# Query, key and value order in group B, and layer 0's key/value projection slice by slice

## The chip, the cores and the metric

The kernel runs on one core of one Trainium2 chip, in one launch. The metric is the device time of a run in microseconds (us), the median of several runs. Five engines work side by side, each through its own queue in order: TensorE (PE in the profile, its weight loads PEld), VectorE (DVE), ScalarE (ACT), GpSimd (POOL) and SyncE (SP), which here only issues DMA transfers. They meet at semaphores.

## The reference

A two-layer encoder on a sequence of 512 tokens and 1024 features, all in float32. A layer is:

```
h = rmsnorm(x, g_attn)
qa, ka, va, qb, kb, vb = split(h @ w_in)          # 512, 128, 128, 512, 512, 512 columns
ya = windowed_attention(rope(norm(qa)), rope(norm(ka)), va, sink)   # 8 heads of 64, 2 kv heads
yb = differential_attention(rope(norm(qb)), rope(norm(kb)), vb)     # 4 heads, two softmaxes each
x = x + concat(ya, rmsnorm(yb)) @ w_out
h = rmsnorm(x, g_ffn)
gate, val = split(h @ w_up)                       # 2 x 2816 columns
x = x + (silu(conv3(gate)) * val) @ w_down
```

## The kernel before, in words

x lies transposed: features on the 128 partitions, in eight slices of 128 (`x_sb[k]`), tokens along the free axis. Every product is made from three float32r products: each operand is split into a high part `hi` (rounded by ScalarE) and a low part `lo` (the rest, by VectorE or GpSimd), and `mm3` (L197 to L200) adds hi·hi, hi·lo and lo·hi in PSUM. Weights come in units of at most 512 KB. `emit_unit` (L176) loads one into `wr`, rounds it into `wh` and writes the rest into `wl`; `next_unit` (L190) keeps the loads three units ahead. There are two buffers `wr` and three each of `wh` and `wl`.

The norm before a projection is not applied to x. `Norm.add` (L212) multiplies a slice by its gain and splits it into `na_h` and `na_l`; `Norm.square` (L221) sums the squares of the slices; `Norm.rms` (L233) sums them over the partitions with plain float32 matmuls (`na_ss`) and GpSimd raises the mean to the power -0.5 (`na_r`, `r_tok`). The scale of a token is multiplied in when a projection's bank is read: `scaled` (L329) for queries and keys, `v_out` (L374) for values.

The input projection of a layer runs in nine chunks of 256 columns (`CHUNKS`, L29): key/value of group A, two of A's queries, and for each half of group B value, query and key. `project` (L315) works through a chunk in two banks of two token tiles each, so 8 x 12 = 96 matmuls. After a bank of queries or keys, `qk_out` (L335) does the head norm and the rotary embedding: ScalarE scales and squares, VectorE sums, GpSimd takes the power, multiplies and adds, TensorE transposes into the one bank `tq`, and ScalarE and VectorE split the result. It works in four shared buffers `rp`. The banks in PSUM are: two `mm`, two `at`, one double bank `sc` for scores, one `acc` and one `tq`.

At the start of layer 0 (L254 to L269) the eight slices of x and the first two weight units are loaded, eight `add` are emitted and then eight `square`: four on GpSimd, four on ScalarE and VectorE. Then come the tables for the rotary embedding (`make_tabs`, on GpSimd) and `rms`, then chunk after chunk.

Attention is a track of its own. `attend` (L592) goes through group A's eight steps (two score groups each), then through eight score steps for each half of B; values follow a step or two behind, and after a half's four value products the outputs are normed (`b_norm`: `ss_yb`, `rt_yb`, both in `tq`). `weave` (L125) interleaves this track with the other one, B's projections (`proj_b`, L629) and the first output projection, by given shares of cost. A track may hand out a condition and is passed over until it holds: B's scores of a half wait for `("done", half)`, set when its projections are emitted. The order in which the instructions then stand in the engines' queues is chosen by a planner from the emission order and its own estimate of times.

The feed-forward part follows (L697 to L741).

Of the kernel before, what the change touches and what calls it, by code (L numbers as in the profile page):

```python
# [10 lines left out]
F32 = mybir.dt.float32  # L11
# [17 lines left out]
CHUNKS = ("akv", "aq0", "aq1", "bv0", "bq0", "bk0", "bv1", "bq1", "bk1")  # L29
# [7 lines left out]
FIRST_SQ = 4  # L37
# [5 lines left out]
def kernel(  # L43
# [102 lines left out]
    ones, nhalf, warm = (unit[:, i:i + 1] for i in range(3))  # L146
    nc.gpsimd.memset(ones, 1.0)
    nc.gpsimd.memset(nhalf, -0.5)

# [26 lines left out]
    def emit_unit():  # L176
# [7 lines left out]
        for o in ([slice(0, k)] if i > 1 else [slice(j, j + 1) for j in range(k)]):  # L184
            nc.scalar.copy(hi[:, o], raw[:, o])  # L185
            eng.tensor_tensor(out=lo[:, o], in0=raw[:, o], in1=hi[:, o], op=ALU.subtract)  # L186
        ready.append((hi, lo))
        state["emitted"] += 1

# [13 lines left out]
    class Norm:  # L203
        def __init__(self, l, base, name):
            self.l, self.base, self.name = l, base, name
            self.first = l == 0 and base == 0
            self.x = []
            self.hi = [None] * NK
            self.lo = [None] * NK
            self.part = [sb.tile([P, S], F32, tag="tab", bufs=3, name=f"{name}_sum")]  # L210
# [10 lines left out]
        def square(self, k):  # L221
            if self.first and k == FIRST_SQ:
                self.part.append(tmp(f"{self.name}_sum2"))
            sq = self.part[-1] if k == 0 or self.first and k == FIRST_SQ else tmp(f"{self.name}_q{k}")
            if self.first and k < FIRST_SQ:
                nc.gpsimd.tensor_tensor(out=sq, in0=self.x[k], in1=self.x[k], op=ALU.mult)
            else:
                nc.scalar.activation(sq, self.x[k], AF.Square)
            if sq is not self.part[-1]:
                eng = nc.vector if self.first and k >= FIRST_SQ else nc.gpsimd  # L230
                eng.tensor_tensor(out=self.part[-1], in0=self.part[-1], in1=sq, op=ALU.add)

        def rms(self):  # L233
            acc = accum(f"{self.name}_ss")
            for t in range(NT):
                for k, sq in enumerate(self.part):
                    nc.tensor.matmul(acc[:, t:t + 1], lhsT=sq[:, t * P:(t + 1) * P], rhs=ones,  # L237
                                     start=k == 0, stop=k == len(self.part) - 1)
# [11 lines left out]
    def split_out(hi, lo, src):  # L250
        nc.scalar.copy(hi, src)
        nc.vector.tensor_tensor(out=lo, in0=src, in1=hi, op=ALU.subtract)
# [18 lines left out]
    for l in range(depth):  # L271
# [36 lines left out]
        r_tok = norm.rms()  # L308
        if l == 0:
            make_tabs((2, 3))  # L310
# [4 lines left out]
        def project(name, done, alloc):  # L315
            w = [next_unit(), next_unit()]
            for tp in range(NT // 2):
                bank = alloc(f"pj{l}_{name}_{tp}").rearrange("p (t c) -> p t c", t=2)
                for i in range(2):
                    t = 2 * tp + i  # L320
                    for k in range(NK):
                        mm3(bank[:, i], (h_in.hi[k][:, t * P:(t + 1) * P], h_in.lo[k][:, t * P:(t + 1) * P]),
# [6 lines left out]
        def scaled(name, bank, tp):  # L329
            raw = rp(name)  # L330
            for i in range(2):
                nc.scalar.activation(raw[:, i], bank[:, i], AF.Copy, scale=r_tok[:, 2 * tp + i:2 * tp + i + 1])
# [56 lines left out]
        run(project("akv", akv_done, turn))  # L389
# [10 lines left out]
        run(proj_a(0, turn))  # L400
        run(proj_a(1, turn))
# [88 lines left out]
        def bv_done(half, bank, tp):  # L490
            v = keep(f"vb{l}_{half}_{tp}")
            vb[half, tp] = (v[:, 0], v[:, 1])
            for i in range(2):
                o = slice(i * CW, (i + 1) * CW)
                v_out(bank[:, i], v[:, 0, o], v[:, 1, o], 2 * tp + i)
# [96 lines left out]
        def attend():  # L592
# [4 lines left out]
            def values():  # L597
# [9 lines left out]
                if qb % 2:  # L607
                    yield from b_values(kind, qb // 2, j)
# [202 lines left out]
```

## Time and profile before

| | |
|---|---|
| median of 3 runs | 1282.15 us (1281.47 to 1282.38) |
| profiled execution | 1282.14 us, span 1280.4 us |
| TensorE busy | 1226.6 us, 96% of the span |
| VectorE, ScalarE, GpSimd busy | 58%, 44%, 28% |
| mean granted TensorE clock | 0.98 of full speed |
| read from memory | 99.73 MB, 80 GB/s over the span |

Busy time of TensorE counts a matmul from its start to its modelled end, and neighbours overlap; the idle time between them is what to look at. In a row of the timeline, the note in brackets is the time for which the engine stood idle before it, and what ended that.

### The profile page before, as it was taken

To read this page: it belongs to the slowest core of one execution; us is meant where nothing else is said; L and a number is where in the kernel's file an instruction comes from. 1 tells how busy PE (TensorE), PEld (TensorE's weight loads), DVE (VectorE), ACT (ScalarE), POOL (GpSimd) and SP (SyncE) were. 2 spreads that over 40 slices of the span, in tenths; PEclk is the share of its full clock that TensorE was granted. 3 is DMA by queue.
4 is the path that set the end of the run, shared out by engine and by line. 5 is a ranking of instruction groups with operands and counts; after the bars stand their busy time and mean duration, and the time that the engine had idled before them with its cause. 6 is when DMAs were issued, how large, how long until landed. Compare 5 with 4: busy or idle time off the path is not lost. (4 is left out here: it accounts for less than half of the span.)

```text
span 1280.4 us, 17034 instructions
## 1 busy us (share of the span) xinstructions
PE 1226.6 (96%) x6648; PEld 1034.8 (81%) x6648; DVE 737.5 (58%) x1181; ACT 569.6 (44%) x1007; POOL 359.2 (28%) x354
## 2 busy tenths in 40 slices
PE   6999996989999999999999999978999999999998
PEld 6988875787888888888899988757888888888887
DVE  6656786767655324554447677766765542355532
ACT  4477854435433223333345877544443332233321
POOL 5756481114211000112146465702421110011100
PEclk8999998899999999999999999979999999999999
DMA  5312120113332233332332112201133323333232
GB/s 176 100 35 66 42 78 22 32 34 100 99 99 87 87 107 99 99 99 72 93 115 67 52 49 67 64 3 37 63 108 106 98 76 99 107 99 99 80 109 91
DMA packets 32752, 102.92 MB, mean 80 GB/s; under 512 B 3872, under 2 KB 4128, under 8 KB 32672
## 3 DMA queue, kind: packets, MB, share of 16 engines
q1 hardware_dynamic: 32672, 101.84, 25.9%
q8 instruction: 52, 0.85, 0.3%
q14 instruction: 28, 0.23, 0.1%
HBM read 99.73 MB, written 2.10 MB: 80 GB/s over the span
## 5 line engine op out<-in xcount | busy, mean ns | idle before, releaser
L185 ACT CAST wh<-wr 128x1024 fp32r<-128x1024 f32 (+3 forms) x210 | 197.8, 945 | 404.0 <-PE up L199 171.0
L199 PE MATMUL up<-nf_l,wh 128*128 128x512 f32 x704 | 274.6, 390 | 0.6 <-DVE nf_l L217 0.5
L200 PE MATMUL up<-nf_h,wl 128*128 128x512 f32 x704 | 274.1, 390 | 0.4
L198 PE MATMUL up<-nf_h,wh 128*128 128x512 f32 x704 | 273.4, 390 | 0.0
L186 DVE TENSOR_TENSOR wl<-wr,wh 128x1024 fp32r<-128x1024 f32 (+3 forms) x174 | 192.2, 1108 | 107.0 <-ACT wh L185 106.7
L717 POOL TENSOR_TENSOR cv<-cv,rb 128x512 f32<-128x512 f32 x44 | 59.2, 1346 | 516.8 <-ACT cv L716 516.8
L199 PEld LDWEIGHTS up<-nf_l,wh 128*128 128x128 f32 x704 | 132.1, 188 | 30.0 <-DVE nf_l L217 2.8
L200 PEld LDWEIGHTS up<-nf_h,wl 128*128 128x128 f32 x704 | 132.2, 188 | 28.5 <-DVE wl L186 1.5
L198 PEld LDWEIGHTS up<-nf_h,wh 128*128 128x128 f32 x704 | 132.1, 188 | 27.6 <-ACT nf_h L216 0.2
L200 PE MATMUL dn<-act,wl 128*128 128x512 f32 x352 | 139.0, 396 | 0.0
L198 PE MATMUL dn<-act,wh 128*128 128x512 f32 x352 | 137.4, 391 | 0.0
L199 PE MATMUL dn<-act,wh 128*128 128x512 f32 x352 | 137.0, 390 | 0.0
L186 POOL TENSOR_TENSOR wl<-wr,wh 128x1024 fp32r<-128x1024 f32 x36 | 86.7, 2411 | 100.3 <-ACT wh L185 100.3
L710 DVE TENSOR_TENSOR gp<-up,rb 128x512 f32<-128x512 f32 x44 | 30.3, 692 | 103.4 <-PE up L200 98.4
L199 PEld LDWEIGHTS dn<-act,wh 128*128 128x128 f32 x352 | 66.1, 188 | 16.1
L200 PEld LDWEIGHTS dn<-act,wl 128*128 128x128 f32 x352 | 66.1, 188 | 14.5
L198 PEld LDWEIGHTS dn<-act,wh 128*128 128x128 f32 x352 | 66.1, 188 | 14.0
L718 DVE TENSOR_TENSOR cv<-cv,up 128x512 f32<-128x512 f32 x44 | 30.2, 687 | 81.4 <-POOL cv L717 72.1
L521 ACT ACTIVATE e_b<-sc_b,mx_b,rqb 128x512 f32<-128x512 f32 x64 | 49.2, 774 | 51.4 <-DVE mx_b L518 51.3
L731 DVE TENSOR_TENSOR x<-x,dn 128x512 f32<-128x512 f32 x32 | 22.0, 687 | 77.2 <-PE dn L200 77.2
L716 ACT ACTIVATE cv<-cv 128x512 f32<-128x512 f32 x44 | 27.7, 631 | 71.6 <-DVE cv L715 71.6
L517 DVE TENSOR_REDUCE mx_b<-sc_b 128x2 f32<-128x1024 f32 x32 | 39.0, 1218 | 7.2 <-PE sc_b L515 7.0
(212 smaller groups left out, 2551.6 us busy)
## 6 DMA issues: line engine op xcount, KB each, us to landing
wr<-w_up SPq DMA_DIRECT2D x88, 512.0 KB, 3.6
wr<-w_in SPq DMA_DIRECT2D x36, 512.0 KB, 3.6
wr<-w_down SPq DMA_DIRECT2D x32, 384.0 KB, 3.0
wr<-w_down SPq DMA_DIRECT2D x32, 320.0 KB, 2.9
wr<-w_out SPq DMA_DIRECT2D x16, 512.0 KB, 3.6
x<-xT SPq DMA_DIRECT2D x8, 256.0 KB, 5.5
outT<-x SPq DMA_DIRECT2D x8, 256.0 KB, 2.0
rows<-row_par SPq DMA_DIRECT2D x2, 260.0 KB, 4.1
```

What stands on the lines that cost most here:

```text
L185: nc.scalar.copy(hi[:, o], raw[:, o])
L186: eng.tensor_tensor(out=lo[:, o], in0=raw[:, o], in1=hi[:, o], op=ALU.subtract)
L198: nc.tensor.matmul(acc, lhsT=a[0], rhs=b[0], start=start, stop=False)
L199: nc.tensor.matmul(acc, lhsT=a[0], rhs=b[1], start=False, stop=False)
L200: nc.tensor.matmul(acc, lhsT=a[1], rhs=b[0], start=False, stop=stop)
L517: nc.vector.tensor_reduce(out=mx, in_=scp, axis=AX, op=ALU.max)
L521: nc.scalar.activation(e[c], sc[c], AF.Exp, bias=mx[:, c:c + 1], scale=rq[:, c:c + 1], accum_out=lsum[:, c:c + 1])
L710: nc.vector.tensor_tensor(out=g[:, 1:S + 1], in0=acc[0], in1=rb, op=ALU.mult)
L716: nc.scalar.activation(cv, cv, AF.Silu)
L717: nc.gpsimd.tensor_tensor(out=cv, in0=cv, in1=rb, op=ALU.mult)
L718: nc.vector.tensor_tensor(out=cv, in0=cv, in1=acc[1], op=ALU.mult)
L731: nc.vector.tensor_tensor(out=x_sb[d], in0=x_sb[d], in1=acc, op=ALU.add)
```

## The change

Two things change.

In each half of B the order is now query, key, value. The condition `("done", half)` is set after the key, and a new one, `("values", half)`, after the value chunk; B's value products wait for it. The columns of `w_in` are laid out in the new order. The fourth chunk of a layer, whose low parts VectorE makes and not GpSimd, is now a query chunk.

In layer 0, x and the weights of the first chunk (A's key/value) are loaded as eight pairs of slices, and the chunk runs slice by slice over all four token tiles in the two `mm` banks, emitted before anything else. As four sums are open in two banks at once, two matmuls of a zero operand clear the banks first. The squares of the first norm get a scale `gate`, which is always 1 but is computed from the low part of the fourth weight unit, so they can't start before it. All eight are now on ScalarE, the sums on VectorE. The sum over partitions is emitted after the first 12 matmuls of the first query chunk, and the key/value banks are read after that. The first query chunk takes the two `at` banks, the second a score bank and one in turn. In layer 1 the first chunks run as before.

```diff
-CHUNKS = ("akv", "aq0", "aq1", "bv0", "bq0", "bk0", "bv1", "bq1", "bk1")
+CHUNKS = ("akv", "aq0", "aq1", "bq0", "bk0", "bv0", "bq1", "bk1", "bv1")
...
+FIRST_MM = 1
...
         def square(self, k):
...
-            if self.first and k < FIRST_SQ:
-                nc.gpsimd.tensor_tensor(out=sq, in0=self.x[k], in1=self.x[k], op=ALU.mult)
-            else:
-                nc.scalar.activation(sq, self.x[k], AF.Square)
-            if sq is not self.part[-1]:
-                eng = nc.vector if self.first and k >= FIRST_SQ else nc.gpsimd
-                eng.tensor_tensor(out=self.part[-1], in0=self.part[-1], in1=sq, op=ALU.add)
+            sq = self.part if k == 0 else tmp(f"{self.name}_q{k}")
+            nc.scalar.activation(sq, self.x[k], AF.Square, **({"scale": gate} if self.first else {}))
+            if k:
+                eng = nc.vector if self.first else nc.gpsimd
+                eng.tensor_tensor(out=self.part, in0=self.part, in1=sq, op=ALU.add)
...
-    nc.sync.dma_start(x_sb[0], x_v[:, 0])
+    first_w = [[sb.tile([P, 4, CW], dt, tag=tag, bufs=b, name=f"{tag}_f{i}")
+                for dt, tag, b in ((F32, "prob", 4), (F32R, "wh", 3), (F32R, "wl", 3))] for i in range(2)]
+    for k in range(NK):
+        nc.sync.dma_start(x_sb[k], x_v[:, k])
+        nc.sync.dma_start(first_w[k // 4][0][:, k % 4], units[k // 4][0][:, k % 4])
+    state.update(emitted=2, used=2)
+    ready.extend([None, None])
+    nc.sync.dma_start(ident, ident_in)
+    norm = Norm(0, 0, "na0")
+    first_banks = []
+    for tp in range(2):
+        b = mm(f"pj0_akv_{tp}")
+        nc.tensor.matmul(b, lhsT=zero.broadcast_to([P, P]), rhs=zero.broadcast_to([P, S]), start=True, stop=False)
+        first_banks += [b[:, i * CW:(i + 1) * CW] for i in range(2)]
+    for k in range(NK):
+        norm.add(k, x_sb[k])
+        raw, hi, lo = (v[:, k % 4] for v in first_w[k // 4])
+        split(nc.vector, hi, lo, raw)
+        for t in range(NT):
+            mm3(first_banks[t], (norm.hi[k][:, t * P:(t + 1) * P], norm.lo[k][:, t * P:(t + 1) * P]),
+                (hi, lo), False, k == NK - 1 and t % 2 == 1)
     emit_unit()
-    for k in range(1, NK):
-        nc.sync.dma_start(x_sb[k], x_v[:, k])
-        if k == 4:
-            emit_unit()
-    nc.sync.dma_start(ident, ident_in)
+    emit_unit()
+    nc.vector.tensor_scalar(out=gate, in0=ready[-1][1][:, 0, :1], scalar1=1.0, scalar2=1.0, op0=ALU.max, op1=ALU.min)
     nc.sync.dma_start(rope_sb, rope)
     nc.sync.dma_start(mask_sb, mask)
-    norm = Norm(0, 0, "na0")
-    for k in range(NK):
-        norm.add(k, x_sb[k])
     for k in range(NK):
         norm.square(k)
...
-        run(proj_a(0, turn))
-        run(proj_a(1, turn))
+        if l:
+            run(proj_a(0, turn))
+        else:
+            p0 = proj_a(0, at)
+            for _ in range(FIRST_MM):
+                next(p0)
+            r_tok = norm.rms()
+            for tp in range(2):
+                akv_done(first_banks[2 * tp:2 * tp + 2], tp)
+                next(p0)
+            make_tabs((2, 3))
+            run(p0)
+        run(proj_a(1, turn if l else lambda nm: (lambda n: sc2(n)[:, 0], turn)[int(nm[-1])](nm)))
...
                 if qb % 2:
+                    yield lambda: ("values", kind) in qk
                     yield from b_values(kind, qb // 2, j)
...
-            yield from project(f"bv{half}", lambda bank, tp: bv_done(half, bank, tp), mm)
             yield from project(f"bq{half}", lambda bank, tp: qk_out(
...
             qk["done", half] = True
+            yield from project(f"bv{half}", lambda bank, tp: bv_done(half, bank, tp), mm)
+            qk["values", half] = True
```

## Rows read from the trace of the kernel before

**Rows 1.** Busy time by stage: length, engines' busy us (instructions), granted clock, DMA share, GB/s

```profile
6.40:31.09 24.69, 20.17 (x112) 18.52 (x113) 18.22 (x25) 11.32 (x22) 16.18 (x16) 0.79 0.49 181
31.09:286.90 255.81, 235.20 (x1619) 204.32 (x1617) 174.78 (x361) 146.90 (x325) 117.03 (x83) 0.95 0.17 51
190.00:245.00 55.00, 42.80 (x221) 32.41 (x221) 36.93 (x67) 24.83 (x54) 11.43 (x7) 0.81 0.10 29
286.90:651.25 364.35, 363.91 (x1601) 298.82 (x1601) 185.36 (x219) 133.53 (x172) 56.26 (x86) 1.00 0.32 96
664.01:908.40 244.39, 226.97 (x1586) 198.33 (x1585) 174.14 (x351) 145.25 (x319) 119.39 (x83) 0.97 0.17 53
826.00:866.00 40.00, 30.25 (x161) 22.91 (x160) 28.57 (x49) 17.32 (x37) 8.03 (x5) 0.83 0.09 27
```

**Rows 2.** Timeline of TensorE, projections of layer 0: start us, us, instruction, tile

```profile
9.70 0.42 PE L198 MATMUL pj_akv<-wh,na_h 128*128 128x256 f32 x1
9.91 0.41 PE L199 MATMUL pj_akv<-wl,na_h 128*128 128x256 f32 x1
...
31.09 0.28 PE L198 MATMUL pj_aq<-wh,na_h 128*128 128x256 f32 x1
31.21 0.28 PE L199 MATMUL pj_aq<-wl,na_h 128*128 128x256 f32 x1
```

**Rows 3.** Busy time by stage, while the first loads run

```profile
4.00:15.00 11.00, 5.86 (x26) 5.03 (x26) 8.91 (x10) 9.43 (x20) 8.39 (x6) 0.97 0.99 374
```

**Rows 4.** Timelines of ScalarE and VectorE, the start of layer 0

```profile
4.76 0.72 ACT L216 ACTIVATE na_h<-x,cols 128x512 fp32r<-128x512 f32 x1 [2.44 <-DMA x<-xT]
5.95 1.32 ACT L185 CAST wh<-wr 128x256 fp32r<-128x256 f32 x4 [0.46 <-DMA wr<-w_in]
7.58 2.74 ACT L216 ACTIVATE na_h<-x,cols 128x512 fp32r<-128x512 f32 x4 [0.31 <-DMA x<-xT]
10.23 0.61 ACT L228 ACTIVATE na_sum<-x 128x512 f32<-128x512 f32 x1
...
5.52 0.81 DVE L217 SCALAR_TENSOR_TENSOR na_l<-x,cols,na_h 128x512 fp32r<-128x512 f32 x1 [5.52 <-ACT na_h L216]
6.38 1.44 DVE L186 TENSOR_TENSOR wl<-wr,wh 128x256 fp32r<-128x256 f32 x4
22.73 0.68 DVE L231 TENSOR_TENSOR na_sum<-na_sum,na_q 128x512 f32<-128x512 f32 x1
30.98 1.23 DVE L186 TENSOR_TENSOR wl<-wr,wh 128x1024 fp32r<-128x1024 f32 x1 [2.50 <-ACT wh L185]
```

**Rows 5.** Timeline of TensorE, plain float32 products of 128 columns

```profile
310.98 1.05 PE L688 MATMUL rps<-ident,nf_r 128*128 128x128 f32 x8
```

**Rows 6.** Timeline of GpSimd, the row scale of layer 0

```profile
29.73 1.03 POOL L248 TENSOR_TENSOR na_r<-na_v,unit 128x4 f32<-128x4 f32 x1
```

**Rows 7.** Timeline of TensorE, the first A scores of either layer

```profile
56.63 0.50 PE L425 MATMUL sc_a<-ka,qah 64*128 64x256 f32 x4
...
684.87 0.51 PE L425 MATMUL sc_a<-ka,qah 64*128 64x256 f32 x4
```

**Rows 8.** Timeline of TensorE, layer 0, from B's half 0 to half 1

```profile
206.06 0.79 PE L515 MATMUL sc_b<-bkh,bqh 64*128 64x512 f32 x2
...
210.75 0.66 PE L370 MATMUL tr_bk<-ident,raw_bk 128*128 128x128 f32 x4 [0.98 <-DVE y_yb L581]
...
213.30 0.79 PE L515 MATMUL sc_b<-bkh,bqh 64*128 64x512 f32 x2
...
218.21 0.50 PE L515 MATMUL sc_b<-bkh,bqh 64*128 64x512 f32 x2 [1.28 <-ACT e_b L521]
```

**Rows 9.** Busy time by stage, and ScalarE's reads of value and query banks

```profile
70.00:100.00 30.00, 28.74 (x223) 25.62 (x223) 18.73 (x54) 25.58 (x62) 16.09 (x11) 1.00 0.24 69
...
62.44 0.47 ACT L375 ACTIVATE vb<-pj_bv,na_r 128x256 fp32r<-128x256 f32 x1 [1.40 <-PE pj_bv L200]
...
82.78 0.83 ACT L332 ACTIVATE raw_bq<-pj_bq,na_r 128x256 f32<-128x256 f32 x2
```

More of the change, by code (lines that the diff above doesn't have):

```diff
@@ L36 @@
 EARLY_IN = 4
-FIRST_SQ = 4
+FIRST_MM = 1
 N_COL = NK + NK + 3 * NF + NF + 1
@@ L145 @@
     unit = const.tile([P, 16], F32, name="unit")
-    ones, nhalf, warm = (unit[:, i:i + 1] for i in range(3))
+    ones, nhalf, warm, gate, zero = (unit[:, i:i + 1] for i in range(5))
     nc.gpsimd.memset(ones, 1.0)
     nc.gpsimd.memset(nhalf, -0.5)
+    nc.gpsimd.memset(zero, 0.0)
     c0 = NK
@@ L183, in emit_unit, with split @@
         eng = nc.gpsimd if kind in ("inb", "out") else nc.vector
-        for o in ([slice(0, k)] if i > 1 else [slice(j, j + 1) for j in range(k)]):
-            nc.scalar.copy(hi[:, o], raw[:, o])
-            eng.tensor_tensor(out=lo[:, o], in0=raw[:, o], in1=hi[:, o], op=ALU.subtract)
+        split(eng, hi, lo, raw)
         ready.append((hi, lo))
         state["emitted"] += 1
+    def split(eng, hi, lo, raw):
+        nc.scalar.copy(hi, raw)
+        eng.tensor_tensor(out=lo, in0=raw, in1=hi, op=ALU.subtract)
     def next_unit():
@@ L209, in __init__ @@
             self.lo = [None] * NK
-            self.part = [sb.tile([P, S], F32, tag="tab", bufs=3, name=f"{name}_sum")]
+            self.first = l == 0 and base == 0
+            self.part = sb.tile([P, S], F32, tag="tab", bufs=3, name=f"{name}_sum")
         def add(self, k, x):
@@ L235, in rms @@
             for t in range(NT):
-                for k, sq in enumerate(self.part):
-                    nc.tensor.matmul(acc[:, t:t + 1], lhsT=sq[:, t * P:(t + 1) * P], rhs=ones,
-                                     start=k == 0, stop=k == len(self.part) - 1)
+                nc.tensor.matmul(acc[:, t:t + 1], lhsT=self.part[:, t * P:(t + 1) * P], rhs=ones,
+                                 start=True, stop=True)
             v = small(f"{self.name}_v", NT)
@@ L318, in project @@
                 bank = alloc(f"pj{l}_{name}_{tp}").rearrange("p (t c) -> p t c", t=2)
+                bank = [bank[:, i] for i in range(2)]
                 for i in range(2):
@@ L331, in scaled @@
             for i in range(2):
-                nc.scalar.activation(raw[:, i], bank[:, i], AF.Copy, scale=r_tok[:, 2 * tp + i:2 * tp + i + 1])
+                nc.scalar.activation(raw[:, i], bank[i], AF.Copy, scale=r_tok[:, 2 * tp + i:2 * tp + i + 1])
             return raw
@@ L387, in akv_done @@
             qk_out(raw[:, :, :P], tp, tabs[1], [v.unsqueeze(1) for v in ka], "ka", None)
-        run(project("akv", akv_done, turn))
+        if l:
+            run(project("akv", akv_done, turn))
         rqa = sb.tile([P, NT, 4, 2], F32, tag="rqa", bufs=1, name=f"rqa{l}")
@@ L494, in bv_done @@
                 o = slice(i * CW, (i + 1) * CW)
-                v_out(bank[:, i], v[:, 0, o], v[:, 1, o], 2 * tp + i)
+                v_out(bank[i], v[:, 0, o], v[:, 1, o], 2 * tp + i)
         b_st = {}
```

18 lines of the change are left out of this document (6 added, 12 removed).

## Prediction, made before the change was run

> **What bounds the kernel now.** I read the busy time by stage first, because the average over the span hides where TensorE stands [rows 1]. In the first feed-forward half TensorE is busy 363.91 of 364.35 us at full clock; layer 1's looks the same, and nothing in this change touches either. Three places leave TensorE time over. From 6.40 to 31.09 us, layer 0's key/value projection, it is busy 20.17 of 24.69 us at a mean granted clock of 0.79, and before 6.40 it does nothing. Layer 0's attention stretch, from the first query matmul at 31.09 to the first up-projection, has 20.6 us idle of 255.81, and 12.2 of these lie between 190 and 245, where the clock is 0.81. Layer 1's has 17.4 us idle of 244.39, 9.75 of them from 826 to 866. Everything that the change can win is in these three places, and TensorE's matmuls elsewhere are the floor. The chain of waits says little here: it ends in down-projection matmuls that wait for nothing.
>
> **Part one, the start of layer 0.** The projection is 4 token tiles x 8 slices x 3 = 96 matmuls of 256 columns. Two levels show: starts 0.21 us apart (9.70, 9.91), which is the 1.2 GHz level, and 0.12 apart (31.09, 31.21), the 2.4 GHz level [rows 2]. So the 96 need 20.2 us at the lower and 11.5 at the upper level. They run until 31.09 today.
>
> What feeds them in the changed kernel: eight pairs of a 256 KB slice of x and a 128 KB slice of weights, 0.39 MB a pair, 3.15 MB. From 4 to 15 us the DMA moved 374 GB/s [rows 3], so a pair lands each 1.05 us and the last at 4.76 + 7 x 1.05 = 12.1. ScalarE rounds a slice of x and one of weights: four of the first take 2.74 us and four of the second 1.32, so 1.02 us a pair, from 4.76 on. VectorE makes the low parts: 0.81 and a quarter of 1.44, so 1.17 us a pair, where GpSimd is nearly idle beside it [rows 4]. GpSimd's squares and sums, which run beside these today, are gone. Eight pairs at 1.17 us from 5.5 end at 14.9. That is faster than TensorE at its lower level (12 matmuls, 2.5 us a pair) and faster than at its upper one (1.44).
>
> The start is then TensorE's. First matmul at about 5.9, 0.5 us earlier than now, since the first weight slice is a quarter of a unit. The two matmuls by zero ahead of it are of a shape that this trace does not show; I bound them between nothing and four of the plain float32 products of 128 columns, of which four (eight records) take 1.05 us at the upper level [rows 5], so 2.1 us each at the lower: 4.2 us from about 1 us on, done before data is there. I cost them at nothing; if they started late, each us would be one of delay. At which clock do the 96 run? At the upper level they end at 5.9 + 11.5 = 17.4, at the lower at 5.9 + 20.2 = 26.1, and at the mean of today's stretch, 0.79 with its waits, at 5.9 + 11.5/0.79 = 20.5. Since the stretch will have fewer waits I take the middle of 17.4 and 20.5, 19.0, and keep the two levels as bounds.
>
> The lower bound is a case of its own: today's stretch, which waits for its slices again and again, has a mean of 0.79 and matmuls 0.21 us apart in it [rows 1, 2]. The Trainium skill, in "TensorE: Matmul & The Clock Gate", section on HAM oscillation, says that a loop whose compute for each slice is shorter than its wait for the next falls back to the lower clock on every slice. By that rule the sum would use 26.1 instead of 19.0, a rival below; here the feed (1.17 us a pair) is the shorter of the two, which speaks against it.
>
> The query projection needs its two weight units rounded: VectorE takes 1.23 us for one [rows 4], so 14.9 + 2.5 = 17.4, ahead of 19.0. On SP's queue these two units now stand ahead of the rotary, mask and parameter rows (0.72 MB); all 5.1 MB take 13.6 us at 374 GB/s, so they are there by some 17 us, ahead of GpSimd's first use that matters, the scale at 27. The query projection starts at 19.0 instead of 31.09: a lead of 12.1 us. The sum over the squares (eight records now, sixteen before) moves behind that start, about 1 us by the same float32 row [rows 5]: lead 11.1.
>
> **What the held-back squares cost.** The gate waits for the low part of the fourth weight unit, 17.4. Then eight squares on ScalarE at 0.61 (4.9 us) and seven sums on VectorE at 0.68 [rows 4], more where GpSimd's tables run beside it; sums done at 23.5 to 26. With TensorE's 1 us and GpSimd's power, 1.03 us [rows 6], the row scale is there at 25.7 to 28.5. I take 27.2, against 30.76 now. So the thing that opens all norm, rotary and attention work moves by only 3.6 us while the projections move by 11.1. Queued behind the scale are the two banks of key/value and the banks of the first query chunk. They are held by extra space (the change gives the second query chunk a score bank), so TensorE goes on meanwhile.
>
> First scores of group A stand at 56.63 [rows 7], 25.9 us after the scale. The chain between (ScalarE, VectorE, GpSimd, with four buffers "rp") stays, less two weight splits of 1.23 us that stand inside it today: 27.2 + 25.9 - 2.5 = 50.6, so 6.0 us earlier. The first scores then come 31.6 us after the first query matmul, where they come 25.5 after it now: attention lags the projections by 6.1 us more. What does lag cost? Layer 1 has 684.87 - 664.01 = 20.9 us of it, 4.6 less than layer 0, and its attention stretch is 11.4 us shorter [rows 1, 7]. Only 3.2 of the 11.4 are idle time (20.6 against 17.4); the rest is mostly the lower clock. Bounds for 6.1 us of lag: nothing (projections fill in, attention catches up) and 11.4/4.6 = 2.5 for one, 15.2 us. I take the idle time alone, 3.2/4.6 = 0.7 for one, 4.3 us, since layer 0 has its low clock now too. Part one: 11.1 - 4.3 = 6.8 us faster, with ends at 11.1 faster and 4.1 slower.
>
> **Part two, the order inside each half of B.** No instruction is added or taken away. Before, key comes last in a half. Its second transpose shares the one bank "tq" with the norm of B's first outputs, whose emission stands ahead of it in the interleaving. So the transposes of half 1 wait at 210.75 for y_yb, and between half 0's last scores at 206.06 and half 1's first at 213.30 lie 7.24 us, while the next scores follow 4.91 us later [rows 8]. With query and key ahead of value, those transposes are emitted before that norm and the gap should shrink to the cadence: 2.3 us less, in each layer (layer 1 repeats the pattern). What is late next is the cadence itself: one score bank, read by VectorE's maximum and ScalarE's exponentials. Total 4.6; I take 4.0 for the two. The other side: key and query chunks now come first, into the stretch where ScalarE is busiest, 25.58 of 30 us from 70 to 100. A value tile takes two ScalarE operations of 0.47 us, a query tile two scalings in 0.83 us plus a square and a rounding [rows 9], about 1.1 us more. Two tiles change places in each half, so if ScalarE were the limit there, 4.4 us per layer would be lost at first, and given back when the value tiles come. Bounds for both layers: 11 us faster (half of the 22 us idle in the two tail stretches goes) to 8.8 slower.
>
> **Sum.** The profiled execution took 1282.14 us for a span of 1280.4, and the median is 1282.15, so no correction. 1282.1 - 6.8 - 4.0 = 1271.3 us. A change within 0.2%, 2.6 us, could not be told from none.
>
> **Rivals.** (a) The lead stays whole: the half of B that TensorE bounds takes up all lag. For it: only 8.4 us of layer 0's idle time lie outside 190 to 245, so TensorE, not attention, sets the pace up to there. Against: the layers differ by 11.4 us. 1282.1 - 11.1 - 4.0 = 1267; with half the tails' idle time gone as well, 1260. (b) Attention sets the end and the order gives nothing: scores 6.0 us earlier, less about 1 us that ScalarE loses. 1277. (c) The clock stays at its lower level through the slices. The projection ends at 26.1, a lead of 5.0 - 1 = 4.0 us, but then the scale is not late for it and no lag is added; with 4.0 from the order 1274. This is what the Trainium skill's rule above would do here, its time worked out from rows. (d) Slower: lag is paid at the rate between the two layers, 2.5 for one. It happens in the tail from 190, where scores follow each other at their own cadence with no projections left to fill, and the clock falls as TensorE idles. At 8 us of lag (the scale at 28.5, and the four rp buffers refilled before the query tiles) it costs 20 against 11.1 + 4.0, 1287. At that rate it decides from (11.1 + 4.0)/2.5 = 6.0 us of added lag, and I forecast 6.1, so only the lower rate keeps it off. Against it: much of the layers' difference is clock, 0.81 over 55 us against 0.83 over 40. (e) The instruction order is made by a planner from its own estimate, so emission order need not be queue order; the new queues could eat what is won. 1282.
>
> **How the numbers follow.** Forecast, 1268 to 1276: 0.38. (a) 0.18, (b) 0.15, (c) 0.10, (d) 0.09, (e) 0.10. Faster by over 0.2%: 0.38 + 0.18 + 0.10 + most of (b) = 0.78. Slower: (d) and a little of (e) = 0.11. Same: the rest, 0.11. Eight times in ten: 1261 to 1282; it takes in (a) nearly to its end, (b) and (c), and leaves out (d) and part of (e).
>
> **What would show it.** The first query matmul at 17 to 21 us, not 31, and the last key/value matmul just ahead of it. Granted clock at 1.00 from about 10 us on; if it is 0.50 through to 25, (c). VectorE's low parts of x all at 0.75 to 0.85 us. The row scale at 26 to 29. First A scores at 48 to 53, so 29 to 33 us after the first query matmul; 34 or more would bring (d). From the last scores of half 0 to the first of half 1 about 5 us in both layers, with no wait of a key transpose for y_yb. Idle of TensorE in layer 0's stretch rising from 20.6 toward 25, in layer 1's falling from 17.4. I am wrong if TensorE stands still for several us behind the sum of squares just after 20 us, or if layer 1's stretch, which sees the order alone, gets longer.

## The result, and the profile after

The changed kernel takes 1272.8 us (median of 4 runs, 1271.91 to 1273.91) where the kernel before takes 1282.22 beside it (1281.47 to 1282.38): a ratio of 0.9928, interval 0.9915 to 0.994, some 9.3 us. The forecast was 1271.3. The sum came out. The experiments below show that several of its terms did not.

The profiled execution took 1273.49 us for a span of 1271.7. First the busy time by stage, columns as in [rows 1]: the key/value projection, layer 0's attention stretch, the part of it from half 0's last scores on, the first feed-forward half, and layer 1's stretch.

```profile
5.50:19.20 13.70, 13.64 (x96) 13.35 (x97) 9.62 (x18) 9.36 (x16) 0.00 (x0) 1.00 0.88 314
19.20:276.49 257.29, 236.07 (x1626) 206.46 (x1625) 173.46 (x374) 152.39 (x334) 123.97 (x93) 0.95 0.17 53
198.21:276.49 78.28, 66.47 (x391) 54.34 (x391) 51.28 (x100) 32.65 (x66) 11.03 (x7) 0.89 0.09 27
276.49:640.39 363.90, 363.45 (x1602) 298.94 (x1601) 185.55 (x219) 133.68 (x172) 56.13 (x86) 1.00 0.32 96
653.15:900.31 247.16, 231.00 (x1585) 200.93 (x1584) 169.19 (x350) 145.67 (x319) 119.14 (x83) 0.94 0.17 52
```

The projection has no hole left (13.64 of 13.70), against 20.17 of 24.69 before. Its granted clock reads 1.00, though the matmuls below stand 0.21 us apart until 9.72. The column counts full speed up to the trace's first record of the clock, which comes at 9.72 here, so at the start of the program the distance between matmuls decides. Layer 0's attention stretch is 1.5 us longer than before, its idle time 21.2 us where it was 20.6. Layer 1's is 2.8 us longer, at a mean clock of 0.94 instead of 0.97 [rows 1]. One execution can be off by some 3 us in such a stretch (last section), so small differences are read from the medians.

TensorE's timeline, from the zero matmuls to B's scores and to layer 1; the columns are those of [rows 2], and the lines answer to [rows 2, 5, 7, 8].

```profile
0.95 3.78 PE L264 MATMUL pj_akv<-unit 128*128 128x512 f32 x4 [0.95 <-POOL unit L149]
...
9.29 0.41 PE L203 MATMUL pj_akv<-wh_f,na_l 128*128 128x256 f32 x1
9.50 0.38 PE L201 MATMUL pj_akv<-wh_f,na_h 128*128 128x256 f32 x1
9.72 0.29 PE L202 MATMUL pj_akv<-wl_f,na_h 128*128 128x256 f32 x1
9.85 0.28 PE L203 MATMUL pj_akv<-wh_f,na_l 128*128 128x256 f32 x1
...
19.20 0.40 PE L201 MATMUL pj_aq<-wh,na_h 128*128 128x256 f32 x2
...
30.48 0.95 PE L234 MATMUL na_ss<-unit,na_sum 128*128 128x1 f32 x8
...
54.55 0.50 PE L447 MATMUL sc_a<-ka,qah 64*128 64x256 f32 x4
...
198.21 0.50 PE L537 MATMUL sc_b<-bkh,bqh 64*128 64x512 f32 x2
...
203.42 0.50 PE L537 MATMUL sc_b<-bkh,bqh 64*128 64x512 f32 x2 [2.72 <-ACT e_b L543]
...
674.00 0.50 PE L447 MATMUL sc_a<-ka,qah 64*128 64x256 f32 x4
```

Three distances are to be read here. The first query matmul stands at 19.20, 11.9 us earlier. The first A scores are only 2.1 us earlier, 35.35 us behind that matmul. Between half 0's last scores and half 1's first lie 5.2 us instead of 7.24, and what is waited for is ScalarE's exponential.

Where the row scale was lost, in the timelines of ScalarE, VectorE and GpSimd [rows 4, 6]:

```profile
16.58 1.05 ACT L190 CAST wh<-wr 128x1024 fp32r<-128x1024 f32 x1 [2.19 <-DMA wr<-w_in]
17.93 1.05 ACT L190 CAST wh<-wr 128x1024 fp32r<-128x1024 f32 x1 [0.30 <-DMA wr<-w_in]
20.96 0.72 ACT L226 ACTIVATE na_sum<-x,unit 128x512 f32<-128x512 f32 x1 [1.98 <-DVE unit L275]
21.59 4.39 ACT L226 ACTIVATE na_q<-x,unit 128x512 f32<-128x512 f32 x7
```

```profile
5.21 0.75 DVE L220 SCALAR_TENSOR_TENSOR na_l<-x,cols,na_h 128x512 fp32r<-128x512 f32 x1 [5.21 <-ACT na_h L219]
...
14.79 0.42 DVE L191 TENSOR_TENSOR wl_f<-prob_f,wh_f 128x256 fp32r<-128x256 f32 x1
17.66 2.58 DVE L191 TENSOR_TENSOR wl<-wr,wh 128x1024 fp32r<-128x1024 f32 x2 [2.45 <-ACT wh L190]
...
20.78 0.14 DVE L275 TENSOR_SCALAR unit<-wl 128x1 f32<-128x1 f32 x1
...
22.33 5.62 DVE L229 TENSOR_TENSOR na_sum<-na_sum,na_q 128x512 f32<-128x512 f32 x7 [0.59 <-ACT na_q L226]
...
31.75 0.15 DVE L237 TENSOR_SCALAR na_v<-na_ss 128x4 f32<-128x4 f32 x1
```

```profile
31.52 0.91 POOL L292 TENSOR_TENSOR tab<-rope_sb,rows 128x256 f32<-128x256 f32 x1 [7.31 <-PE na_ss L234]
32.39 0.87 POOL L296 TENSOR_TENSOR tab<-rope_sb,rows 128x128 f32<-128x128 f32 x2
33.22 1.01 POOL L245 TENSOR_TENSOR na_r<-na_v,unit 128x4 f32<-128x4 f32 x1
```

The two query units are split at 20.24. The gate (the one-element operation on `unit`) releases the squares at 20.96, and the sums end at 27.95. Then the sum over partitions waits in TensorE's queue behind query matmuls until 30.48, and the power waits in GpSimd's behind a table's products until 33.22. GpSimd had stood idle for 7.31 us ahead of that table: the table takes a buffer in which the sums of the squares still lay, so it too was set free by the sum over the partitions, and it stands ahead of the power in the queue. The scale is there at 34.23: 3.5 us later than before, not 3.6 earlier.

### The profile page after: what moved, and what is told of

It reads as the page before. It is cut to its first block, busy times and chain, and to the rows that moved or that the text cites. A ratio compares the mean times of both kernels' runs of the same rounds, so it can differ in the third digit from the quotient of the medians.

```text
span 1271.7 us, 17055 instructions
## 1 busy us (share of the span) xinstructions
PE 1228.0 (97%) x6644; PEld 1035.9 (81%) x6644; DVE 722.4 (57%) x1186; ACT 573.5 (45%) x1011; POOL 348.6 (27%) x348
## 5 line engine op out<-in xcount | busy, mean ns | idle before, releaser
L190 ACT CAST wh<-wr 128x1024 fp32r<-128x1024 f32 (+2 forms) x202 | 195.0, 967 | 401.6 <-PE up L202 171.4
L191 DVE TENSOR_TENSOR wl<-wr,wh 128x1024 fp32r<-128x1024 f32 (+2 forms) x166 | 185.5, 1118 | 105.9 <-ACT wh L190 105.6
L202 PE MATMUL dn<-act,wh 128*128 128x512 f32 x352 | 136.3, 388 | 0.0
```

What stands on the lines that cost most here:

```text
L190: nc.scalar.copy(hi, raw)
L191: eng.tensor_tensor(out=lo, in0=raw, in1=hi, op=ALU.subtract)
L202: nc.tensor.matmul(acc, lhsT=a[0], rhs=b[1], start=False, stop=False)
```

## The experiments

The times of two kernels are compared through their ratios to the kernel before, which ran beside each; 0.001 is 1.28 us.

| kernel | median us | ratio [95%] | first A scores | first up-projection | between |
|---|---|---|---|---|---|
| before | 1282.22 | 1 | 56.63 | 286.80 | 230.2 |
| after | 1272.8 | 0.9928 [0.9915, 0.994] | 54.55 | 276.49 | 221.9 |
| e1 start only | 1279.89 | 0.9974 [0.9965, 0.9983] | 52.20 | 282.69 | 230.5 |
| e2 order only | 1278.19 | 0.9964 [0.9952, 0.9976] | 57.65 | 284.11 | 226.5 |
| e3 order in layer 0 only | 1272.42 | 0.9913 [0.9898, 0.9927] | 53.96 | 273.75 | 219.8 |
| e4 no gate | 1269.68 | 0.9891 [0.9878, 0.9904] | 49.20 | 275.82 | 226.6 |
| e5 e1, key transposes in `mm` | 1285.2 | 1.0016 [1.0007, 1.0025] | 54.39 | 285.66 | 231.3 |
| e6 later gate | 1274.71 | 0.9928 [0.9915, 0.994] | 54.26 | 275.51 | 221.3 |
| e7 no gate, late tables | 1266.71 | 0.9876 [0.9861, 0.9891] | 47.51 | 272.41 | 224.9 |
| e8 after, more zeros (one run) | 1269.45 | none | 52.30 | 272.58 | 220.3 |
| e9 no gate, old order | 1264.7 | 0.9858 [0.9843, 0.9873] | 49.28 | 269.25 | 220.0 |
| e10 e7, more zeros | 1267.85 | 0.9874 [0.9859, 0.9889] | 47.42 | 272.49 | 225.1 |
| e11 query, value, key | 1277.13 | 0.9949 [0.9937, 0.9962] | 54.32 | 283.49 | 229.2 |
| e12 e9, late tables | 1264.06 | 0.987 [0.9848, 0.9892] | 47.27 | 268.67 | 221.4 |

The last three columns are us of layer 0 in the profiled execution. (One of e10's four executions took 3062.57 us and one of e3's six 1721.93; nothing in the traces here explains them. The ratios leave them out, the medians don't: without them e10's is 1267.32 and e3's 1271.59.)

**The two parts alone.** e1 keeps the new start and puts the old order back (`VFIRST` names the layers with values first); e2 is the kernel before with the new order; e3 has the new order in layer 0 alone.

```diff
+            if l in VFIRST:
+                yield from project(f"bv{half}", lambda bank, tp: bv_done(half, bank, tp), mm)
+                qk["values", half] = True
             yield from project(f"bq{half}", lambda bank, tp: qk_out(
...
-            yield from project(f"bv{half}", lambda bank, tp: bv_done(half, bank, tp), mm)
-            qk["values", half] = True
+            if l not in VFIRST:
+                yield from project(f"bv{half}", lambda bank, tp: bv_done(half, bank, tp), mm)
+                qk["values", half] = True
```

Expected of e1: 

> The start of layer 0 as changed, but value, query, key in each half of B in both layers, as before the change. Theory of the prediction: the start alone gives 6.8 us and the order 4, so 1275.4 us. Rival, read from the trace of the changed kernel: the start gives nearly all of its lead of 11.9 us and the order costs about 3 us a layer, so 1267 to 1270 us, faster than the whole change. Layer 1's stretch from the first query matmul to the first up-projection would be 244.2 us as before the change, against 247.2 in the changed kernel.

Expected of e2: 

> The start of layer 0 as before, but query, key, value in each half of B in both layers. Theory of the prediction: 4 us faster than before, 1278 us. Rival: the order costs 3 us in layer 1 and about as much in layer 0, 1285 to 1288 us. If it costs in layer 1 alone, 1285 us. The gap from the last scores of half 0 to the first of half 1 is about 5.2 us in both theories; what differs is whether the stretch of layer 1 is shorter or longer than 244.2 us.

Expected of e3: 

> The changed start, query, key, value in layer 0 alone; layer 1 has value, query, key. Rival theory: layer 1 goes back from 247.2 to 244.2 us, so 3 us less than the changed kernel, 1269.8 us. Theory of the prediction (the order gains 2 us a layer): 1274.8 us. Against the kernel with the start alone it shows what the order is worth in layer 0 with the new start: the prediction's theory has it 2 us faster than that kernel, the rival 0 to 3 us slower.

The start alone is worth 3.3 us, the order alone 4.6, the order in layer 0 on top of the new start 7.8 (0.9974 to 0.9913). Both theories had e1 faster than it was, and neither gave the order so much in layer 0. e2 came out as the prediction's theory had it. In layer 1 the order is worth nothing that can be told (e3 against after, intervals overlapping). e1 against e3 shows where layer 0's part lies, as both come to B's half 0 at the same time. Busy time by stage of e1, from the first query matmul on: to the first A scores, to half 0's first scores, to its last, to half 1's first, to its last, to the up-projection. Under it the same half 0 of e3.

```profile
18.34:52.20 33.86, 31.44 (x260) 30.66 (x258) 25.04 (x45) 18.43 (x35) 22.83 (x25) 1.00 0.31 93
52.20:143.26 91.06, 85.17 (x633) 76.39 (x632) 64.22 (x160) 67.29 (x160) 52.27 (x36) 0.96 0.18 55
143.26:199.28 56.02, 51.04 (x330) 43.09 (x329) 43.14 (x69) 34.23 (x76) 38.17 (x26) 0.96 0.20 60
199.28:208.18 8.90, 8.04 (x41) 6.79 (x41) 6.46 (x14) 4.13 (x9) 1.02 (x1) 0.65 0.01 2
208.18:251.04 42.86, 35.04 (x179) 26.51 (x180) 28.47 (x50) 18.61 (x41) 5.78 (x3) 0.84 0.06 16
251.04:282.69 31.65, 28.03 (x188) 25.56 (x189) 19.31 (x41) 9.62 (x17) 4.39 (x3) 0.95 0.14 45
```

```profile
143.28:195.33 52.05, 50.13 (x334) 42.34 (x333) 38.99 (x72) 32.95 (x71) 27.78 (x18) 1.00 0.21 63
```

Half 0 itself is 4.0 us shorter in e3, with 1.9 us of TensorE's time idle instead of 5.0, a clock of 1.00 instead of 0.96, and VectorE and GpSimd less busy; the gap behind it is 5.2 instead of 8.9. So the order's gain is half outside the gap that the forecast had named. And e1's gap is hardly a wait: TensorE is busy for 8.04 of its 8.90 us, at a clock of 0.65.

**Is it the wait in `tq`?** e5 keeps e1's order but gives half 1's key transposes another bank. e11 has the order query, value, key in layer 0: the key comes last as before, the value no longer first.

```diff
-            tr = tq(f"tr_{nm}")[:, :nb * CW].rearrange("p (b q) -> p b q", b=nb)
+            tr = (mm if nm.startswith("bk1") else tq)(f"tr_{nm}")[:, :nb * CW].rearrange("p (b q) -> p b q", b=nb)
```

```diff
             yield from project(f"bq{half}", lambda bank, tp: qk_out(
...
+            if l not in VFIRST:
+                yield from project(f"bv{half}", lambda bank, tp: bv_done(half, bank, tp), mm)
+                qk["values", half] = True
             yield from project(f"bk{half}", lambda bank, tp: qk_out(
...
-            yield from project(f"bv{half}", lambda bank, tp: bv_done(half, bank, tp), mm)
-            qk["values", half] = True
```

Expected of e5: 

> The start alone (old order in both layers), but the key transposes of half 1 go to a bank mm instead of tq, so that they no longer wait for the norm of B's first outputs. Theory of the prediction (the order wins because these transposes waited): the gap from half 0's last scores to half 1's first falls from 8.9 to about 5.2 us in layer 0 and from 5.7 to about 5 in layer 1, and the kernel comes near what the order gave: 1280 minus 4 to 6, 1274 to 1276 us. Rival (the order wins because the heavy query and key tiles leave the stretch of half 0's scores, which takes 56.0 us in the start alone and 52.1 with the new order): half 0 stays at 56 us, and at most the gap's 3.7 us are won, or less, 1277 to 1280 us.

Expected of e11: 

> New start. In layer 0 the order inside a half is query, value, key (key last, as in the old order; query first, as in the new one); layer 1 keeps the old order. It stands beside two kernels already timed that differ from it in layer 0's order alone: value, query, key at 1279.9 us and query, key, value at 1272.4. Theory A (the key's transposes wait because they come last): with key last again the gap between half 0's last scores and half 1's first is 8 to 9 us as in the old order, and the time is 1278 to 1281. Theory B (what counts is that value tiles, light for ScalarE, no longer come first and that heavy query tiles get out of half 0's scores): a query chunk stands first, the key's chunk falls into half 0's scores; half 0's scores are shorter than the old order's 56 us by some 2, and the time is half-way, 1275 to 1277. Theory C (anything but value first will do): 1272 to 1274 with a gap of about 5 us.

e5 is 5.4 us slower than e1, where both of its forecasts had it faster. Its timeline of TensorE between the halves of layer 0 shows no wait at all: the gap of 8.7 us is full of value and output products, which now stand ahead of the scores.

```profile
201.31 0.50 PE L538 MATMUL sc_b<-bkh,bqh 64*128 64x512 f32 x2
...
204.96 0.48 PE L202 MATMUL wo<-yh,wh 128*128 128x512 f32 x1
...
209.97 0.50 PE L538 MATMUL sc_b<-bkh,bqh 64*128 64x512 f32 x2
```

Most of what e5 loses lies, by its profile, in layer 1, whose transposes the edit moves as well. There the gap is 18.8 us where e1 has 5.7, with the key's transposes only at 839.10, behind value products, and the stretch takes 251.6 us where e1's takes 245.2.

```profile
825.02 0.50 PE L538 MATMUL sc_b<-bkh,bqh 64*128 64x512 f32 x2 [0.80 <-ACT e_b L544]
...
843.81 0.50 PE L538 MATMUL sc_b<-bkh,bqh 64*128 64x512 f32 x2
```

So e5 changed more than the wait, and it doesn't show what the wait alone costs. e11's time, 1277.13, is that of theory B, half-way; but B's own mark failed, since half 0's scores take 56.6 us there and not 54. The key transposes do wait, as TensorE's timeline of e11 has it, with a gap of 6.8 us:

```profile
207.63 0.66 PE L381 MATMUL tr_bk<-ident,raw_bk 128*128 128x128 f32 x4 [0.78 <-DVE y_yb L604]
```

These two runs narrow nothing down to a single wait.

**The gate.** e4 is the changed kernel without the scale on the squares; e6 lets a third weight unit be emitted ahead of the gate, which is then taken from that unit.

```diff
-    nc.vector.tensor_scalar(out=gate, in0=ready[-1][1][:, 0, :1], scalar1=1.0, scalar2=1.0, op0=ALU.max, op1=ALU.min)
...
-            nc.scalar.activation(sq, self.x[k], AF.Square, **({"scale": gate} if self.first else {}))
+            nc.scalar.activation(sq, self.x[k], AF.Square)
```

```diff
     emit_unit()
     emit_unit()
+    emit_unit()
     nc.vector.tensor_scalar(out=gate, in0=ready[-1][1][:, 0, :1], scalar1=1.0, scalar2=1.0, op0=ALU.max, op1=ALU.min)
```

Expected of e4: 

> The changed kernel with the squares not held back: the scale by the gate is left out, so the planner may put the squares anywhere. In the changed kernel the row scale is there at 34.2 us and the first A scores stand at 54.55. Theory that lag of attention costs 0.7 us for one: if the scale comes about 6 us earlier and the slices are not delayed, 1268.5 us. Rival: the eight squares (0.62 us each) go between the slices on ScalarE and put off the projection by up to 5 us, its end going from 19.2 to 22 to 24 us, so 1273 to 1277 us. Third: the lag costs nothing and the slices are not delayed, 1272.8 us.

Expected of e6: 

> The changed kernel with the squares held back further: the gate comes from the low part of the fifth weight unit instead of the fourth. Theory that the first A scores, and so the row scale, set the end one for one while the projections' lead is worth nothing by itself: the scale moves from 34.2 to about 40 us, the first scores from 54.6 to about 60, and the time from 1272.8 to about 1278 us. Theory of the prediction (0.7 for one): 1277 us. Rival (attention catches up, lag is free): 1272.8 us.

Without the gate the kernel is 4.7 us faster than after (0.9928 to 0.9891). The first A scores come 5.3 us earlier, and the squares fit between ScalarE's roundings at the price of 2 us in the projection (its last matmul at 21.09). The scale comes 6.5 us earlier (27.77), so by ratio the gain is the 0.7 for one of the forecast. The profiled executions don't show it where it was expected: e4 reaches the first up-projection 0.7 us before after, and another 2.9 lie in layer 1 (244.25 us against 247.16, at a clock of 0.97 against 0.94). e6 gave no dose: the power started 1.2 us later (34.40), the first A scores not at all, and its ratio is that of after.

**How early, and in which order.** e7 has no gate, the new order in layer 0 alone, and the tables of the second pair held behind the row scale. e9 has no gate and the old order in both layers, and e12 is e9 with the late tables.

```diff
+            one = small("one", 1)
+            nc.vector.tensor_scalar(out=one, in0=r_tok[:, :1], scalar1=1.0, scalar2=1.0, op0=ALU.max, op1=ALU.min)
+            nc.vector.tensor_scalar(out=rows[:, 2 * HD:4 * HD], in0=rows[:, 2 * HD:4 * HD], scalar1=one, scalar2=None,
+                                    op0=ALU.mult)
             make_tabs((2, 3))
```

Expected of e7: 

> What the runs so far point to: the changed start without the gate, the tables for group B made to come after the row scale on GpSimd (in the kernel without the gate three tables stand ahead of the power from 19.2 to 26.8 us, while its operand is there at 22.2), query, key, value in layer 0 alone. If the first scores set the end one for one: the scale at about 25.3 instead of 27.8, first scores at about 47 instead of 49.2, so 2 us less than the kernel without the gate (1269.7), 1267.5 us; layer 1's old order adds 0 to 2 us of gain, 1266 to 1267.5 us. If the slices are by now what limits: 1269 to 1270 us.

Expected of e9: 

> New start without the gate on the squares, old order (value, query, key) in both layers. Theory A (layer 0's end follows the first A scores one for one, and the order is worth its own 4.6 to 7 us whatever the start): the first A scores come at about 49 us as in the kernel without a gate, so 3.2 us ahead of the gated start with the old order (1279.9 us): 1275 to 1277. Theory B (the order's gain is only the room that a late start takes from half 0, and an earlier start gives it by itself): 1270 to 1272, as the new order has it without a gate (1269.7).

Expected of e12: 

> The fastest kernel so far (new start without the gate, old order in both layers, 1264.7 us, row scale's power at 26.85 us, first A scores at 49.28) with the second pair of rotary tables held behind the row scale, which brought the power from 26.76 to 24.05 and the first A scores from 49.20 to 47.51 in the new order. Theory A (layer 0's end follows the first A scores one for one): first A scores at 47.5 and 1263.0 us. Theory B (what decides is how the instructions of the attention stretch fall in the queues, and each change of the start draws a new arrangement worth several us either way): the first A scores again at 47.5, but the time is off 1263 by more than 2 us, either way, and TensorE's stretch from half 0's first scores to the first up-projection, 134.6 us in the kernel it starts from, changes by as much.

The late tables do what they should (GpSimd's timeline of e7), and e7's time is in the range that its first theory gave:

```profile
24.05 1.02 POOL L246 TENSOR_TENSOR na_r<-na_v,unit 128x4 f32<-128x4 f32 x1
```

e9 was forecast wrong by both theories, and it is the run that teaches most. With the old order it is 4.2 us faster than e4 with the new one (0.9858 against 0.9891, intervals apart). Taking the gate away is worth 4.7 us in the new order and 14.9 in the old (e1 against e9). The order, worth 4.6 to 7.8 us of gain with a late scale, gains nothing with an early one. What it costs there is less sure. e4 and e9 differ in layer 1's order too, though their profiled executions differ in layer 0 (first up-projection 6.6 us apart, layer 1's stretch 244.3 and 244.7 us). e7 and e12 differ in layer 0's order alone, and their ratios can't be told apart (0.9876 and 0.987), with medians 2.7 us apart. Busy time by stage of e9, in the same six steps as e1 above:

```profile
18.97:49.28 30.31, 29.02 (x241) 28.51 (x239) 20.24 (x35) 13.23 (x27) 25.41 (x25) 1.00 0.28 88
49.28:134.62 85.34, 83.76 (x648) 75.50 (x647) 58.74 (x163) 66.89 (x162) 53.17 (x36) 1.00 0.21 64
134.62:190.31 55.69, 54.30 (x355) 46.00 (x354) 41.37 (x73) 35.50 (x75) 39.29 (x27) 0.98 0.21 61
190.31:196.43 6.12, 3.49 (x25) 2.60 (x24) 3.50 (x7) 3.21 (x7) 0.62 (x1) 0.93 0.00 0
196.43:239.25 42.82, 36.81 (x197) 28.01 (x197) 29.40 (x57) 20.17 (x42) 5.90 (x4) 0.88 0.08 25
239.25:269.25 30.00, 26.50 (x177) 23.92 (x177) 17.58 (x36) 9.18 (x16) 4.83 (x3) 0.94 0.11 36
```

The second line against e1's is the largest difference: from the first A scores to half 0, TensorE is idle for 1.6 us instead of 5.9 and its clock is 1.00 instead of 0.96, 5.7 us in all. e1's stops there and in half 0 are, in TensorE's timeline:

```profile
130.55 0.58 PE L202 MATMUL pj_bq<-wh,na_h 128*128 128x256 f32 x1 [2.45 <-DVE vb L387]
...
194.78 0.50 PE L538 MATMUL sc_b<-bkh,bqh 64*128 64x512 f32 x2 [4.47 <-ACT e_b L544]
```

And e9, by ratio the fastest of all, still has the very wait that the order was to remove:

```profile
194.31 0.66 PE L380 MATMUL tr_bk<-ident,raw_bk 128*128 128x128 f32 x4 [1.17 <-DVE y_yb L603]
```

e12 brings the first A scores 2.0 us further forward and half 0's first scores 2.2 (132.38), and gives most of it back later: its stretch from there to the up-projection is 136.3 us against 134.6. Half 1, from its first scores to its last, takes 3.1 us more than in e9's fifth line above (busy time by stage of e12):

```profile
192.75:238.63 45.88, 40.09 (x198) 30.92 (x198) 30.12 (x57) 20.06 (x42) 7.03 (x4) 0.78 0.08 24
```

From half 1's first scores on, the two traces show the same instructions in the same order on all four engines, and the same long waits. What differs is the granted clock, 0.78 against 0.88. So these 3.1 us don't come of another arrangement, as theory B would have it. e12's median is 1.1 us from theory A's 1263.0, and its executions lie between 1263.46 and 1269.36, so A is not refuted. By ratio e9 and e12 can't be told apart; both beat the changed kernel by some 8 us.

**The clock at the start.** e8 is the changed kernel, and e10 is e7, with each zero matmul issued twice.

```diff
-        nc.tensor.matmul(b, lhsT=zero.broadcast_to([P, P]), rhs=zero.broadcast_to([P, S]), start=True, stop=False)
+        for i in range(2):
+            nc.tensor.matmul(b, lhsT=zero.broadcast_to([P, P]), rhs=zero.broadcast_to([P, S]), start=True, stop=i == 0)
```

Expected of e8: 

> The changed kernel with each of the two matmuls by zero issued twice, so that TensorE is busy without a gap until data comes. In the changed kernel the two run from 0.95 to 4.73, the first of the 96 at 5.52, and these stand 0.16 to 0.21 us apart until about 9.3, 0.12 after. If what TensorE did before sets the clock of the slices: the 0.12 level comes earlier, by 7 us, and the last of the 96 ends 1 to 2 us earlier than 19.2 although the zero matmuls end later (8 us at most, if at the lower level throughout). If not: the 96 start about 2 us later and end at 20 to 21 us.

Expected of e10: 

> The fastest kernel so far (no gate on the squares, the tables of the second pair behind the row scale, new order in layer 0 alone, 1266.7 us) with each of the two matmuls of zeros issued twice, so that TensorE is busy until about 7 us instead of 4.7 before the projection's matmuls. If TensorE's activity ahead of the first slices sets when the granted clock rises: matmuls 0.12 us apart from about 8 us on instead of 9, and the last key/value matmul up to 1 us earlier. If the end then follows the projections: 1266; if it follows the first A scores, which hang on the row scale and not on the projections: 1266.7 as before, first A scores within 0.5 us of 47.5. If the added 2.3 us of zeros push the first slices' matmuls back: 1267.5 or more.

e8's single run gave 1269.45 us. Its timeline of TensorE:

```profile
3.67 3.99 PE L265 MATMUL pj_akv<-unit 128*128 128x512 f32 x5
7.10 0.80 PE L201 MATMUL pj_akv<-wh_f,na_h 128*128 128x256 f32 x2
7.74 0.28 PE L202 MATMUL pj_akv<-wl_f,na_h 128*128 128x256 f32 x1
7.86 0.28 PE L203 MATMUL pj_akv<-wh_f,na_l 128*128 128x256 f32 x1
```

With zeros until the first slice the spacing is 0.12 from 7.74 on, 2.0 us before after's 9.72. But the projection starts 1.6 us later, so the first query matmul comes at 19.01 instead of 19.20. e10 against e7 is no difference (0.9874 and 0.9876). A single run says nothing of e8's time.

That more zeros brought the upper level forward is not shown either, because other runs reach it earlier with the two zero matmuls of after. TensorE's timelines of e1 and of e10:

```profile
6.58 0.28 PE L204 MATMUL pj_akv<-wh_f,na_l 128*128 128x256 f32 x1
```

```profile
0.95 5.09 PE L266 MATMUL pj_akv<-unit 128*128 128x512 f32 x8 [0.95 <-POOL unit L150]
```

From 6.58 on e1's matmuls stand 0.13 us apart or less wherever none waits. e10's eight records of zeros take 5.09 us where e8's take 6.71, so there the upper level came while only zeros had run. In e3, which starts as after does, it was there at 7.47, and from 8.08 to 11.48 the matmuls stood 0.21 apart once more. The same start thus meets the clock at different times in different executions, and e8's 2.0 us are no more than that spread.

## Why the prediction was right, and where only its sum was

**The lead: right.** First query matmul 19.20, forecast 19.0, and the last key/value matmul just ahead of it. The low parts took 0.75 and 0.42 us, as expected. The clock reached its upper level at 9.72, after 3.8 us of zero matmuls and 4 us of the projection itself, and stayed; the 96 ran at 0.21 apart before and at 0.12 after. The zero matmuls took 3.78 us from 0.95, within the bounds, and were done before the data; in e10 the upper level came while only zeros had run, which the forecast did not count. That 19.20 lies so near to 19.0 is in part luck. With the same first chunk the first query matmul came at 18.31 (e6) to 20.10 us (e3). And the 0.79 that went into the forecast is the column's, which counts full speed at the start [rows 1], where matmuls stood 0.21 apart [rows 2]. Rival (c) did not come: after has no fall between slices, and e3's single one, 16 matmuls at 0.21 instead of 0.12, cost about 1.5 us. The rule named beside it (the Trainium skill, "TensorE: Matmul & The Clock Gate", HAM oscillation) asks for a wait for each slice that is longer than its work, and this trace has none. The sum over partitions took 0.95 us of TensorE, forecast 1; TensorE did not stand still for it.

**The row scale: wrong by 7.0 us,** 34.23 for 27.2. The failed step is the sum from the fourth weight unit's low part at 17.4, over the sums done at 23.5 to 26, to a scale at 25.7 to 28.5. The weights were split 2.8 us later, because they landed later, behind x and the first chunk: the DMA moved 314 GB/s meanwhile, where the forecast had 374. The rest was left out: 2.5 us in TensorE's queue and 1.3 in GpSimd's. The step counted durations and not what stands ahead in the two queues. GpSimd's part could have been read in the kernel before, where the power's operand is there at 28.47 and the power stands behind a table until 29.73 [rows 6]. Without the gate (e9) the scale comes at 27.87, by chance close to what was forecast for the gated one.

**The price of the lag: wrong as a size, and as a kind of term.** The lag from first query matmul to first A scores became 35.35, not 31.6, in the range that was to bring rival (d). e1, the start alone, has 8.3 us more lag than before and a layer 0 stretch longer by 8.6 (264.35 for 255.71), 1.0 for one where the forecast had 0.7 and (d) 2.5; so the start gave 3.3 us, not 6.8. But e9 has 4.8 us more lag than before and a stretch of 250.28, shorter by 5.4. No price for one us of lag holds both. The 4.6 us of lag from which the price was worked out depend on where one counts from: 664.01 is the first query matmul behind layer 1's last key/value matmul, but three others stand at 656.76, and from there layer 1's lag is 28.1 us, more than layer 0's. Rival (b)'s rule that the first A scores set the end fits e1 ("between" in the table 230.5 us, 230.2 before) and not the others: that column runs from 219.8 to 231.3 us, as far as the scores move (47.3 to 57.7). What happens behind the first scores is worth as much as when they come.

**The order: right in size, wrong in place and reason.** 4.6 us alone, forecast 4.0. It should have come from the gap in both layers, 2 us each. The gap did shrink, 7.24 to 5.2 in layer 0 [rows 8], to the cadence as forecast; in layer 1 it had been 5.68 (832.83 to 838.51), not a repeat of 7.24, and is now 5.17. Layer 1 gave nothing. Its stretch was 2.8 us longer, which is the point by which the prediction called itself wrong; but e2 and e4, with the same order there, take 243.7 and 244.3 us, so the order costs nothing there either. In layer 0 half of the gain is in half 0 itself. The lesson of e9 is that the order gains only where the scale is late; the two parts were added in the forecast as if each had a value of its own. The forecast's "other side", heavy tiles moved to where ScalarE is busiest, fits a part of the loss in e4 against e9 (first A scores to half 0: 87.2 us, 49.20 to 136.37, against 85.3) but was not isolated; the larger part of the 6.6 us in layer 0 lies in half 0 itself (58.3 against 55.7) and behind the gap.

**Why the sum came out.** The start gave 3.5 us less than forecast; the order, on the late scale that the start itself brought, gave 5.9 (e1 to after by ratio) and not 4.0. Two errors of opposite sign left 1.5 us, and that is luck.

**What stays open.** Why layer 0 takes 220 us from its first A scores in e9 and 230 in e1 was not found. e5 and e11 isolate no wait; e9 has the wait that the order was to remove and is the fastest by ratio, so that wait alone is not it. Over layer 0's stretch TensorE is idle for 25.6 us at a mean clock of 0.94 in e1, and for 16.4 us at 0.97 in e9. That the planner's arrangement of the queues is the cause is argued, not shown. The clock is a rival that no run sets apart: it alone is seen to differ where e12 and e9 are 3.1 us apart.

## What to carry to other kernels

Price a moved step by what stands ahead of it in its queue at the new time, not by its own duration: here 3.8 us of a 7 us error were two short operations behind others whose results were not due yet. An operation that opens all later work should not be held back for the sake of the engine it shares, before it is measured what it opens. And two edits whose effects go through the same stage are not to be added: test each with and without the other, as the order's gain here was gone once the scale came early.

## What was not expected of the hardware

TensorE's clock can rise while it multiplies nothing but zeros (e10), and one and the same start meets it at different times: matmuls 0.12 to 0.13 us apart from 6.58 in e1 and from 9.72 in after, where in the kernel before they still stood 0.21 apart at 9.70 [rows 2]. The same program's executions differ: e3's ran from 1267.88 to 1274.46, where 16 of the kernel before lie between 1280.92 and 1284.32. In layer 0, where all four engines have the same instructions in the same order in e3 and in after, the two profiles come to the first up-projection 2.7 us apart, with a mean clock of 0.96 and 0.95 over the stretch; one profile settles no stage to less than that. While the eight pairs of slices came in, the weights in pieces of 128 KB, the DMA moved 314 GB/s over the whole projection.
